# Two recurrence streams at a later scheduling priority, and one projection step moved, in a two-layer mixer kernel on one core

## Chip, cores and metric

The kernel runs on one core of a Trainium2 chip. The metric is device time in microseconds, one launch from start to end; "before" is 2253.34 us, the median of three runs (2252.33 to 2256.01). TensorE is called PE below, VectorE DVE, ScalarE ACT, GpSimd POOL and SyncE SP, as in the profile. Nearly all DMAs stand on SP's queue.

## What is computed

The reference is a diffusion backbone of two layers over 512 latent tokens with 256 context tokens ahead of them (768 in all), width 1024, in float32. Cut to what matters here:

```python
for l in range(2):
    h = modulate(rms_norm(x, g_norm1[l]), sh1, sc1)        # latent; hc the same for the context
    proj = h @ w_in[l]                                     # 3744 columns, split into three groups
    # A: latent attention (cq, ckv, kr), 4 heads; B: differential attention (dq, dk, dv), 4 heads
    # C: gated linear recurrence, 8 heads of 64, forward and backward:
    #    S_t = diag(f_t) S_{t-1} + k_t^T v_t ,  o_t = S_t^T q_t   (hf, hb -> f, k; hq -> q; hi -> v)
    x = x + gt1 * (concat(A, B, C * silu(hg)) @ w_out[l])
    x = x + gt2 * swiglu(modulate(rms_norm(x, g_norm2[l]), sh2, sc2))
    # layer 0 does the same for the context tokens, layer 1 does not
return rms_norm(x, g_final)
```

## The kernel before, in words

Products are made from pairs of high and low halves: `gemm` (line 190) issues three matmuls for each 128 rows of weights, weight high by activation high and low, weight low by activation high. Weights come by DMA into `wst`, ACT makes `whi` of it (line 97) and DVE `wlo` (line 100).

In each layer `phase_a` mixes the tokens, and then an FFN follows. `phase_a` is written as generators, which the loop at its end (lines 1036 to 1059) steps in turn by a table of due times:

- `stream_g` projects the columns in the steps of `G_ORDER[l]`: `t0` to `t3` (`trio`) project the forget and query columns of one pair of recurrence heads each and store them to `scr_z`; `h0`, `h1` project the recurrence's token-major inputs (`hi`, the values, line 493) for two pairs each and store them to `scr_v`; `q` and `d` belong to the differential attention; `g0` to `g3` are the output gates, `a4` to `a9` blocks of the modulation. Then it does the output projection (`m2` and `xT` loads, `g<-m` matmuls), whose first part needs the key `"h"`, which is set when the recurrences have ended.
- `stream_p` makes the operands of the latent attention, `stream_a` the attention itself: scores (line 764), a minimum per row on DVE (`mx`, line 768), the exponential on ACT, transposes (line 804), and the product with the values (line 817).
- `stream_h(0)` and `stream_h(1)`, called `h` and `i` in the table, compute the recurrence. Four pairs of heads go one after the other, the first head of a pair in `h` and the second in `i`. A pair loads its inputs from `scr_z` into `hin`, and goes through seven levels (`LEVELS`). Each level makes a masked copy `kz` of `KK` on ACT, twelve (in layer 1 eight) 64x64 score matmuls on PE (line 918, line 930 at the last level), two predicated copies of the scores into `sc` on DVE (line 963), and four products on `KK` and `QQ` on DVE (line 100), on which the next level of the same head stands. Then come transposes of `KK` (line 984), products with the values `hv` (line 990) and a scan over chunks, and the outputs `mixh` (line 1008). `KK`, `QQ` and `sc` have one buffer for each stream, so a pair can't begin before the one ahead of it has ended; the values of `h0` are needed only behind the levels.

The generators set the order in which instructions are recorded. A scheduler then orders each engine's queue: every instruction gets a number, `tc.cur_priority`, which grows by one with each; among instructions that it holds to be ready it takes the lowest number. Each engine runs its list in that order. The scheduler's idea of when something is ready is its own; the hardware waits by semaphores.

The program prints the functions of the change below.

Of the kernel before, what the change touches and what calls it, by code (L numbers as in the profile page):

```python
# [31 lines left out]
GROUPS = ((4, 4, 4, 4, 3, 3), (4, 4, 4, 4, 3, 3))  # L32
LEVELS = (1, 2, 4, 8, 16, 32, 64)
PRED = (1, 2, 4, 8, 16)
G_ORDER = ("t0 h0 q t1 d t2 h1 t3 a5 a4 g0 a8 a6 g1 a9 a7 g3 g2", "t0 t1 h0 t2 q d h1 t3 g0 g1 g3 g2")


PRM = ((40, 2, 2.1, 2, 1.2), (45, 1.8, 2.7, 2.2, 0.4))
# [15 lines left out]
LAG = 4  # L54
LOCK = 1
GB = 1
NSTEP = "011"


# [31 lines left out]
def build(tc, I, out):  # L91
# [304 lines left out]
    def hpair():  # L396
        return (hp.tile([128, KT, T], F32R, tag="hh", name="hh"), hp.tile([128, KT, T], F32R, tag="hl", name="hl"))
# [13 lines left out]
    def phase_a(l, h, fs):  # L411
# [92 lines left out]
        def stream_g():  # L504
# [72 lines left out]
            for i in range(2):  # L577
                steps[f"h{i}"] = partial(hi, i)
            for key in G_ORDER[l].split():
                yield from steps[key]()  # L580
# [152 lines left out]
        def stream_a(at):  # L733
# [47 lines left out]
            def finish(it):  # L781
# [10 lines left out]

                if "h" in done or "proj" in done and GB:
                    bank = cbank if "h" in done else gbank
# [240 lines left out]
        with ps:  # L1035
            vt = {"g": 0.0, "h": 0.0, "i": 0.0, "p": PRM[l][0], "a": 1e9}
            apool = ExitStack()
            gens = {"g": stream_g(), "h": stream_h(0), "i": stream_h(1),
                    "p": stream_p(apool.enter_context(tc.tile_pool(name=f"P{l}", bufs=1, reuse_waits="tile")))}
            stretch = dict(zip("ghipa", (PRM[l][i] for i in (1, 2, 2, 3, 4))))  # L1040
            while gens:
                k = min(gens, key=lambda n: vt[n])
                try:
                    c = next(gens[k])
                except StopIteration:
                    del gens[k]
                    if k == "a":
                        apool.close()
                        done.add("a")
                    if k == "p":  # L1050
                        apool.close()
                        gens["a"] = stream_a(apool.enter_context(tc.tile_pool(name=f"at{l}", bufs=1, reuse_waits="tile")))
                        vt["a"] = vt["p"]
                    continue
                if c == "wait":
                    vt[k] = min(vt[o] for o in gens if o != k) + 1e-3
                else:
                    vt[k] += c * stretch[k]
            apool.close()
# [3 lines left out]

    FIRST = {"q": [O_DQ, O_DQ + 128, O_DK], "t": [O_HF, O_HB, O_HQ]}[G_ORDER[0][0]]
    h = hpair()
# [114 lines left out]
    for l in range(DEPTH):  # L1180
# [3 lines left out]
        po = 0 if full else 256  # L1184
        with ExitStack() as fs:
            x, h2 = phase_a(l, h, fs)
            pbs.close()
            pq = fs.enter_context(tc.tile_pool(name=f"pq{l}", bufs=4, space=PSUM))
# [6 lines left out]
            def ada_next():  # L1195
                for ll, nb in [(0, 10), (0, 11)] + [(1, nb) for nb in range(12)]:
                    if f"{'ab'[ll]}{nb}" in " ".join(G_ORDER).split():
                        continue
# [217 lines left out]
            for n in GROUPS[l]:  # L1416
# [40 lines left out]
                for pcols in ((c,) for c in batches) if last else (parts,):  # L1457
# [13 lines left out]
                    if last:  # L1471
                        if full:
                            if pcols[0].start == 0:
# [3 lines left out]
                                h = hpair()  # L1477
                            norm = norm_mod(x, acc, a1, mod[1][:, 0:8, :], pcols[0], h, wp2, qbank,
                                            lambda: pf.tile([128, 512], F32, tag="f", name="f"), 4, THR if pcols[0] is B1 else "")
                            if pcols[0] is B2:  # L1480
                                for i, (slot, c0) in enumerate(((0, O_HF), (4, O_HB), (8, O_HQ))[:NBEG]):
                                    for _ in range(int(NSTEP[i])):
                                        next(norm)
# [47 lines left out]
```

## Time and profile before

| | value |
|---|---|
| median of three runs | 2253.34 us |
| the profiled execution | 2252.72 us |
| its span, first to last instruction | 2250.8 us |
| PE busy | 2062.0 us (92%) |
| PE weight loads busy | 1764.9 us (78%) |
| DVE busy | 1606.0 us (71%) |
| ACT busy | 1060.6 us (47%) |
| mean granted PE clock | 0.949 |

The span falls into a head (up to about 50 us), the mixing of layer 0 (to about 735), its FFN (to about 1318), the mixing of layer 1 (to about 1850) and its FFN. A view by stretches gives, for each engine, the busy time in that stretch and the number of instructions in brackets; behind them stand the granted PE clock (1.00 is 2.4 GHz, 0.50 is 1.2 GHz, a value between them a mixture), the busy share of the DMA engines and what they moved. Matmuls overlap in the records, so the busy time of PE is more than its work. One 64x64 fp32 matmul is two records.

### The profile page before, as it was taken

Reading aid. Unit: us, or ns where it says so; the run is one execution under the profiler, and the core shown is the slowest. Engines: PE = TensorE matmul, PEld = TensorE weight load, DVE = VectorE, ACT = ScalarE, POOL = GpSimd, SP = SyncE. Lnnn points to the kernel's source line nnn. Section 1 sums busy time; section 2 is a strip of 40 time slices with the busy share of each in tenths; the row PEclk is TensorE's granted clock in tenths of the full one; section 3 lists DMA queues with packets and bytes.
Section 4 is the critical chain, followed back from the end, with each engine's and each line's share of the span. In section 5 each row is a group of like instructions: output and inputs, shape, how many; then the busy total and the mean of one; then the engine's idle time right before and its main releaser. Section 6 shows DMA issues by size and latency. Waiting matters only on the chain.

```text
span 2250.8 us, 38089 instructions
## 1 busy us (share of the span) xinstructions
PE 2062.0 (92%) x14863; PEld 1764.9 (78%) x14863; DVE 1606.0 (71%) x3395; ACT 1060.6 (47%) x1888; POOL 13.2 (1%) x48
## 2 busy tenths in 40 slices
PE   6999999878889999999999999987998679999998
PEld 4887878656577888898999978766876568899997
DVE  5675587867466656687867777788578658777887
ACT  4443776565554322232323453545677444344443
POOL 0000000000000000000000000000000000000000
PEclk9999999878889999999999999998998789999999
DMA  9427643355684433544522342355654553333322
GB/s 310 135 70 176 183 117 116 88 150 158 197 251 136 150 103 113 154 133 140 159 67 70 85 140 83 104 125 140 163 148 127 157 161 104 99 95 107 100 87 69
DMA packets 321244, 296.52 MB, mean 132 GB/s; under 512 B 28875, under 2 KB 263721, under 8 KB 321065
## 3 DMA queue, kind: packets, MB, share of 16 engines
q1 hardware_dynamic: 321064, 294.10, 44.9%
q8 instruction: 117, 1.92, 0.4%
q14 instruction: 63, 0.51, 0.1%
HBM read 241.09 MB, written 52.95 MB: 131 GB/s over the span
## 4 chain that ended last, share of the span: by engine, by line
PE 64%; DVE 13%; ACT 6%; DMA 4%; issue 2%; SPq 0%; DVEq 0%; ACTq 0%
PE g L190 19%; PE q L190 18%; PE f L190 11%; PE b L764 3%; PE g L493 2%; DVE QQ L100 2%; DVE KK L100 2%; DVE sc L963 2%; PE c L918 1%; PE b L190 1%; PE b L817 1%; PE b L804 1%; ACT P L97 1%; DVE mx L768 1%; DMA q<-scr_d 1%
## 5 line engine op out<-in xcount | busy, mean ns | idle before, releaser
L97 ACT ACTIVATE whi<-wst 128x1024 fp32r<-128x1024 f32 (+2 forms) x248 | 225.3, 908 | 413.0 <-PE f L190 143.6
L100 DVE TENSOR_TENSOR wlo<-wst,whi 128x1024 fp32r<-128x1024 f32 (+2 forms) x248 | 255.9, 1034 | 72.3 <-ACT whi L97 67.5
L190 PE MATMUL q<-hh,whi 128*128 128x384 f32 (+1 forms) x708 | 223.6, 318 | 4.3 <-ACT whi L97 3.2
L190 PE MATMUL q<-hh,wlo 128*128 128x384 f32 (+1 forms) x708 | 221.5, 315 | 0.9 <-DVE wlo L100 0.9
L190 PE MATMUL q<-hl,whi 128*128 128x384 f32 (+1 forms) x708 | 221.9, 315 | 0.0
L190 PE MATMUL g<-hh,whi 128*128 128x512 f32 (+1 forms) x560 | 204.8, 367 | 14.4 <-ACT zt L97 6.5
L190 PE MATMUL g<-hl,whi 128*128 128x512 f32 (+1 forms) x560 | 201.0, 360 | 0.4 <-DVE hl L103 0.3
L190 PE MATMUL g<-hh,wlo 128*128 128x512 f32 (+1 forms) x560 | 199.6, 359 | 1.2 <-DVE wlo L100 1.2
L768 DVE TENSOR_REDUCE mx<-b 128x1 f32<-128x768 f32 (+1 forms) x120 | 101.1, 848 | 72.4 <-PE b L764 71.1
L190 PEld LDWEIGHTS q<-hh,whi 128*128 128x128 f32 x708 | 134.3, 191 | 14.2 <-ACT whi L97 6.7
L190 PE MATMUL f<-ah,whi 128*128 128x512 f32 (+1 forms) x380 | 137.2, 364 | 6.4 <-DVE xT L103 4.1
L190 PE MATMUL f<-ah,wlo 128*128 128x512 f32 (+1 forms) x380 | 136.0, 361 | 1.1 <-DVE wlo L100 1.1
L190 PE MATMUL f<-al,whi 128*128 128x512 f32 (+1 forms) x380 | 136.5, 361 | 0.0
L190 PEld LDWEIGHTS q<-hh,wlo 128*128 128x128 f32 x708 | 134.4, 191 | 2.5 <-DVE wlo L100 1.6
L190 PEld LDWEIGHTS q<-hl,whi 128*128 128x128 f32 x708 | 134.6, 191 | 1.2 <-issue 0.8
L190 PEld LDWEIGHTS g<-hh,whi 128*128 128x128 f32 x560 | 109.6, 196 | 32.1 <-ACT zt L97 8.0
L103 DVE SCALAR_TENSOR_TENSOR xT<-f,mod,xT 128x256 f32<-128x256 f32 (+1 forms) x164 | 85.8, 546 | 68.3 <-PE f L190 68.0
L190 PE MATMUL g<-m,whi 128*128 128x256 f32 (+1 forms) x512 | 117.7, 324 | 11.5 <-DMA m<-scr_m 9.4
L97 ACT ACTIVATE kz<-KK 64x384 f32<-64x384 f32 (+1 forms) x192 | 90.9, 475 | 73.6 <-DVE KK L100 35.1
L918 PEld LDWEIGHTS c<-QQ,kz 128*64 128x64 f32 x1920 | 74.0, 153 | 63.3 <-ACT kz L97 34.0
L918 PE MATMUL c<-QQ,kz 128*64 128x64 f32 x1920 | 87.3, 243 | 39.0 <-DVE sc L963 25.9
L190 PEld LDWEIGHTS g<-hh,wlo 128*128 128x128 f32 x560 | 108.8, 195 | 17.1 <-DVE wlo L100 2.3
(308 smaller groups left out, 5103.2 us busy)
## 6 DMA issues: line engine op xcount, KB each, us to landing
wst<-in_w_in_dram SPq DMA_DIRECT2D x58, 512.0 KB, 5.2
wa<-in_w_ada_dram SPq DMA_DIRECT2D x56, 512.0 KB, 3.6
wst<-in_w_out_dram SPq DMA_DIRECT2D x32, 512.0 KB, 4.3
wst<-in_w_ffn_down_dram SPq DMA_DIRECT2D x64, 256.0 KB, 2.9
wst<-in_w_ffn_gate_dram SPq DMA_DIRECT2D x26, 512.0 KB, 3.7
wst<-in_w_ada_dram SPq DMA_DIRECT2D x24, 512.0 KB, 4.7
hin<-scr_z SPq DMA_DIRECT2D x48, 192.0 KB, 3.9
k<-scr_k SPq DMA_DIRECT2D x16, 576.0 KB, 4.8
```

Source lines behind the costliest of these rows:

```text
L97: return S.activation(out=out, in_=in_, func=func, **kw)
L100: eng.tensor_tensor(out=out, in0=in0, in1=in1, op=op)
L103: return V.scalar_tensor_tensor(out=out, in0=in0, scalar=scalar, in1=in1, op0=op0, op1=op1)
L190: PE.matmul(out=o, lhsT=x[:, k, ms], rhs=y[:, k, cols], start=start and k == 0 and p == 0, stop=stop and k == nk - 1 and p == 2, skip_grou ...
L493: PE.matmul(out=o, lhsT=x[:, kk, tok], rhs=y[:, kk % 4, :], start=kk == 0 and p == 0, stop=kk == KT - 1 and p == 2)
L764: PE.matmul(out=s[:, 256 + k0:256 + k0 + kn], lhsT=qq[:, q0:q0 + 128], rhs=kk[:, k0:k0 + kn], start=p == 0, stop=p == len(passes) - 1)
L768: V.tensor_reduce(out=mx, in_=sv, axis=AX.X, op=ALU.min)
L804: PE.transpose(b[:, (kt - k0) * 128:(kt - k0 + 1) * 128], P[:, kt * 128:(kt + 1) * 128], ident)
L817: PE.matmul(out=o[e * 64:e * 64 + 64, :256], lhsT=it["v"][:, e, kt, :], rhs=u[e][:, kt, :], start=kt == 0, stop=kt == it["ntk"] - 1)
L918: PE.matmul(out=bv[e * 64:e * 64 + 64, i, :], lhsT=kz[:, cc], rhs=q[:, cc], start=True, stop=True)
L963: V.copy_predicated(out=sv, data=bv, mask=masks[:64, PRED.index(m), :].unsqueeze(1).to_broadcast([64, n, 64]))
```

## The change

The recurrences' generators `h` and `i` run with `cur_priority` raised by 200 for what they record, in both layers, so that 200 places' worth of other instructions recorded behind them go first where the scheduler holds both ready. When a generator ends, the exception skips the line that takes the 200 off again, so all that is recorded behind the end of `h`, and again of `i`, stands 200 further back as well. In layer 0's table, `h0` stands behind `d` and no longer behind `t0`, so `q`, `t1` and `d` go ahead of it.

```diff
-G_ORDER = ("t0 h0 q t1 d t2 h1 t3 a5 a4 g0 a8 a6 g1 a9 a7 g3 g2", "t0 t1 h0 t2 q d h1 t3 g0 g1 g3 g2")
+G_ORDER = ("t0 q t1 d h0 t2 h1 t3 a5 a4 g0 a8 a6 g1 a9 a7 g3 g2", "t0 t1 h0 t2 q d h1 t3 g0 g1 g3 g2")
...
+AHEAD = ({'h': -200, 'i': -200}, {'h': -200, 'i': -200})
...
                 k = min(gens, key=lambda n: vt[n])
                 try:
+                    p0 = tc.cur_priority
+                    tc.cur_priority = p0 - AHEAD[l].get(k, 0)
                     c = next(gens[k])
+                    tc.cur_priority += AHEAD[l].get(k, 0)
                 except StopIteration:
```

No instruction is added or removed but for 6 of 30 loads of an ACT table, which fall away with the new order. The line numbers of the changed kernel are 1 higher from line 57 on, and 4 higher behind the loop.

The order at three places follows (of each queue, the program's own list; names carry buffer numbers, "x12" is twelve in a row).

PE, layer 0, fourth pair of recurrence heads, in the middle of its levels, before (`QQ_5029` is the first head, `QQ_5056` the second; `kz8` and `kz16` are the levels of 8 and 16):

```order
L804 MATMUL b_5260<-ident_73,P_5148 128x128 x6
L764 MATMUL b_5268<-k_5244,q_5246 128x256
L764 MATMUL b_5268<-k_5244,q_5246 128x512
L918 MATMUL c_5350<-QQ_5029,kz8_1077 64x64 x12
L764 MATMUL b_5394<-k_5244,q_5246 128x256
L764 MATMUL b_5394<-k_5244,q_5246 128x512
L918 MATMUL c_5373<-QQ_5056,kz8_1077 64x64 x12
L190 MATMUL g_5456<-hh_95,whi_5427 128x256
L190 MATMUL g_5456<-hl_96,whi_5427 128x256
L918 MATMUL c_5496<-QQ_5029,kz16_1135 64x64 x12
L918 MATMUL c_5519<-QQ_5056,kz16_1135 64x64 x12
```

The same pair in the changed order (`QQ_4978` and `QQ_5153`):

```order
L919 MATMUL c_5357<-QQ_5153,kz2_788 64x64 x12
L311 MATMUL g_5689<-sel_76,zt_5687 128x2 x4
L304 MATMUL g_5767<-wst_5765,csil_84 32x512
L223 MATMUL b_5494<-blk_77,sq_5492 128x2 x2
L304 MATMUL g_5767<-wst_5765,csil_84 32x512
L304 MATMUL g_5767<-wst_5770,csil_84 32x512 x2
L919 MATMUL c_5517<-QQ_4978,kz16_1044 64x64 x12
L304 MATMUL g_5767<-wst_5774,csil_84 32x512 x2
L304 MATMUL g_5767<-wst_5778,csil_84 32x512 x2
L919 MATMUL c_5540<-QQ_5153,kz4_913 64x64 x9
L311 MATMUL g_5784<-sel_76,zt_5782 128x2 x4
L919 MATMUL c_5540<-QQ_5153,kz4_913 64x64 x3
```

Before, the two heads go side by side, level by level, with little between them; now the second head runs two levels behind the first, and work of other streams stands between nearly all groups.

SP, layer 0, where the first part of the output projection loads its inputs, before (`m2` are the mixers' outputs, `xT` the residual):

```order
L178 DMA wst_6652<-in_w_out_dram 128x8x128
L400 DMA m2_6656<-scr_m0 128x2x512 x2
L400 DMA k_6455<-scr_d0 96x2x768
L400 DMA q_6457<-scr_d0 96x2x256
L178 DMA wst_6654<-in_w_out_dram 128x8x128
L400 DMA zt_6414<-scr_n0 128x768
L400 DMA m2_6656<-scr_m0 128x2x512 x4
```

And in the changed order:

```order
L401 DMA k_6451<-scr_d0 96x2x768
L401 DMA q_6453<-scr_d0 96x2x256
L401 DMA scr_n0<-mixh_5792 128x768
L179 DMA wst_6935<-in_w_out_dram 128x8x128
L401 DMA zt_6410<-scr_n0 128x768
L401 DMA m2_6652<-scr_m0 128x2x512 x3
```

The first two loads of `m2` stood ahead of the last attention head's `k` and `q`; now all eight stand behind them, closer together, and behind the store of the last recurrence's output (`mixh`).

PE, layer 1, last pair of recurrence heads (`QQ_17047` first, `QQ_17110` second), around the level of 4, before:

```order
L764 MATMUL b_15959<-k_15914,q_15916 128x256
L764 MATMUL b_15959<-k_15914,q_15916 128x512
L918 MATMUL c_17346<-QQ_17110,kz4_13137 64x64 x8
L190 MATMUL g_17389<-hh_12393,wlo_17386 128x512
L190 MATMUL g_17389<-hh_12393,whi_17385 128x512
L190 MATMUL g_17389<-hl_12394,whi_17385 128x512
```

and in the changed order (`QQ_17043`, `QQ_17106`):

```order
L805 MATMUL b_16209<-ident_73,P_16162 128x128 x6
L919 MATMUL c_17269<-QQ_17106,kz2_12972 64x64 x8
L919 MATMUL c_17288<-QQ_17043,kz4_13133 64x64 x8
L919 MATMUL c_17342<-QQ_17106,kz4_13133 64x64 x8
L919 MATMUL c_17361<-QQ_17043,kz8_13173 64x64 x8
L765 MATMUL b_16240<-k_16236,q_16238 128x256
```

Before, each group stood alone, with 22 rows of projections and attention between the two heads' groups of the level of 4; now the pair has moved back, and four of its groups follow each other.

## Rows read from the trace of the kernel before

**Rows 1.** The page: span and busy time of PE.

```profile
span 2250.8 us, 38089 instructions
PE 2062.0 (92%) x14863; PEld 1764.9 (78%) x14863; DVE 1606.0 (71%) x3395; ACT 1060.6 (47%) x1888; POOL 13.2 (1%) x48
```

**Rows 2.** View by stretches, both mixing stages: busy time of each engine, clock, DMA.

```profile
core 0: us, PE busy (x) PEld busy (x) DVE busy (x) ACT busy (x) POOL busy (x), PEclk, DMA share, GB/s
...
269.10:312.50 43.40, 39.73 (x476) 32.69 (x473) 41.84 (x81) 34.15 (x62) 0.58 (x4) 1.00 0.42 108
312.50:372.30 59.80, 57.22 (x524) 49.35 (x525) 40.99 (x121) 41.46 (x89) 0.00 (x0) 0.94 0.48 136
372.30:410.50 38.20, 30.50 (x409) 26.10 (x404) 36.72 (x79) 22.23 (x47) 0.59 (x4) 0.92 0.18 59
410.50:477.70 67.20, 58.69 (x471) 42.37 (x471) 46.78 (x132) 45.26 (x82) 0.00 (x0) 0.88 0.52 145
477.70:537.30 59.60, 46.05 (x440) 35.00 (x436) 49.75 (x98) 30.30 (x56) 0.58 (x4) 0.70 0.34 100
537.30:592.00 54.70, 50.69 (x414) 35.68 (x412) 28.28 (x81) 31.57 (x59) 0.00 (x0) 0.97 0.64 187
592.00:631.00 39.00, 32.44 (x153) 21.03 (x153) 19.14 (x35) 20.52 (x38) 0.00 (x0) 0.82 0.90 267
...
1353.40:1385.70 32.30, 27.79 (x307) 22.84 (x302) 30.65 (x80) 14.58 (x31) 0.58 (x4) 0.98 0.20 61
1385.70:1457.10 71.40, 70.54 (x542) 59.05 (x542) 44.03 (x116) 31.52 (x64) 0.00 (x0) 0.96 0.34 96
1457.10:1493.90 36.80, 34.72 (x317) 26.24 (x318) 34.06 (x73) 16.61 (x34) 0.58 (x4) 0.99 0.61 142
...
1528.60:1631.20 102.60, 93.73 (x794) 80.69 (x794) 71.07 (x154) 60.74 (x109) 0.58 (x4) 0.92 0.55 144
1631.20:1689.30 58.10, 55.10 (x419) 42.20 (x421) 43.64 (x115) 43.10 (x74) 0.00 (x0) 1.00 0.56 155
1689.30:1736.10 46.80, 38.46 (x346) 29.42 (x342) 41.21 (x100) 32.44 (x60) 0.58 (x4) 0.85 0.43 127
```

**Rows 3.** Timeline of PE, 395 to 412 us: start, time, instruction, wait before it.

```profile
398.10 0.92 PE L918 MATMUL c<-QQ,kz 128*64 128x64 f32 x24
398.95 0.50 PE L190 MATMUL g<-hl,whi 128*128 128x512 f32 x1
...
401.60 0.92 PE L918 MATMUL c<-QQ,kz 128*64 128x64 f32 x24 [1.91 <-DVE sc L963]
404.93 1.55 PE L918 MATMUL c<-QQ,kz 128*64 128x64 f32 x24 [2.41 <-DVE sc L963]
408.97 1.55 PE L918 MATMUL c<-QQ,kz 128*64 128x64 f32 x24 [2.50 <-ACT kz L97]
```

**Rows 4.** DVE groups, 262 to 592 us: busy, mean ns of one, idle before them.

```profile
L100 DVE TENSOR_TENSOR KK<-KK,tot 64x384 f32<-64x384 f32 x72 | 39.7, 551 | 3.3 <-ACT kz L97 1.4 <-PE c L930 0.4
L100 DVE TENSOR_TENSOR QQ<-QQ,tot 64x384 f32<-64x384 f32 x72 | 39.5, 548 | 0.5
L963 DVE COPY_PREDICATED sc<-masks,c 64x384 f32<-64x384 uint8 x60 | 35.2, 587 | 1.7
L768 DVE TENSOR_REDUCE mx<-b 128x1 f32<-128x768 f32 x32 | 30.4, 955 | 15.6 <-PE b L764 15.1
...
L100 DVE TENSOR_TENSOR wlo<-wst,whi 128x1024 fp32r<-128x1024 f32 x10 | 12.2, 1222 | 6.3 <-ACT whi L97 6.2
```

**Rows 5.** The chain that ended last: start, time, what.

```profile
457.71 2.70 DMA scr_z<-zt
460.97 8.04 DMA hin<-scr_z
...
569.78 2.74 PE b L817 x24
...
1957.41 4.32 PE q L190 x36
...
1999.17 21.92 PE f L190 x96
```

## Prediction

> **What bounds the kernel now.** I read the page first. PE is busy for 2062.0 of 2250.8 us [rows 1], so at first sight order can give little. But the records of matmuls overlap, and a half clock makes them longer, so I priced PE's list instead: 21.92 us for 96 matmuls of 512 columns is 0.228 us each, 4.32 us for 36 of 256 columns is 0.120, and 2.74 us for the 12 value products of two heads (24 records) is 0.23 [rows 5]. Twelve 64x64 scores take 0.92 us with their tail [rows 3]; I take 0.06 each, and price other shapes by their columns in the same way. "Priced us" below are sums of such prices along PE's list. By them the whole list is some 1810 us, so about 440 us of the span are waits, slower clock and latency, and they lie mostly in the two mixing stages.
>
> Second, the view by stretches, cut where the score groups of the recurrence pairs stand: from the first group of the level of 1 to the last of the level of 32. In layer 0 these are 269.1 to 312.5 us (second pair), 372.3 to 410.5 (third) and 477.7 to 537.3 (fourth) [rows 2]. In the third, DVE is busy for 36.72 of 38.2 us and PE's list holds 24.5 priced us; in the fourth it is 49.75 of 59.6, with 27.2 priced us, and the granted clock is 0.70 [rows 2]. In layer 1 the pairs' stretches show the same: 30.65 of 32.3 us, 34.06 of 36.8, and 41.21 of 46.8 for the last [rows 2]. So while a pair goes through its levels DVE bounds the kernel, and PE is under-used. Outside them it is the other way: between 312.5 and 372.3 us PE is busy for 57.22 of 59.8 us, and DVE for 40.99 [rows 2].
>
> Third, the timeline shows how. PE waits 1.91, 2.41 and 2.50 us ahead of three score groups in a row, each time for the recurrence's own work on DVE or ACT [rows 3]. One level of one head costs DVE two predicated copies of 0.587 us, two products on `KK` of 0.551 and two on `QQ` of 0.548 [rows 4], 3.4 us in all; fourteen of them are 47 us, though a pair's first and last lie partly outside the cut.
>
> **The change, part by part.** It adds no work, so what counts is how much other work stands between a pair's groups. From the two orders, between the first and the last group of line 918: the second pair of layer 0 has 34.0 priced us before and 33.2 now, the third 24.5 and 40.2, the fourth 27.2 and 56.0. The fourth has 117 matmuls of other streams before and 281 now. With them DVE work moves in. Summing DVE's rows in the same pieces of the order by their mean durations (a maximum is 0.955 us, a `wlo` 1.222 [rows 4], and so on) gives 44.8 us and 48.9 for the second pair, 40.3 and 61.4 for the third, 53.4 and 72.7 for the fourth.
>
> How long does such a stretch take? Before, the sums of 44.8, 40.3 and 53.4 took 43.4 (269.1 to 312.5), 38.2 and 59.6 us [rows 2]: 1.02 us for 1 us of DVE sum over the three. So now 50, 63 and 74 us: together 46 us more. (PE's work in them, 33 to 56 priced us, is below that.) Against it 43.7 priced us leave the rest of the stage. What they cost there is the largest unknown. In the stretch from 312.5 to 372.3, 48.9 priced us take 59.8, which is 1.22 us for one; from 410.5 to 477.7, 41.0 take 67.2, or 1.64, and from 537.3 to 631 57.2 take 93.7, or 1.64 [rows 2]. At 1.22 they give back 53 us, a net of -7; at 1.64 72 us, a net of -26. The slower stretches hold waits that don't go with the work: a store of 2.70 us and a load of 8.04 ahead of the fourth pair [rows 5], DMA at 0.90 of its engines from 592 to 631 [rows 2]. I take -17, the middle.
>
> Three edits cost nothing by this count. The first pair of layer 0 grows from 40.1 to 44.4 priced us and from 43.9 to 51.2 of DVE, and what it gains it pays. `h0` moved behind `d`: its matmuls run at PE's pace wherever they stand; the first pair's outputs now wait for it (place 219 in PE's priced list, before 115), and the second pair begins at 235 and not 207. That is 28 priced us later, under which `q`, `t1` and `d` run, which had to run anyway. Six fewer ACT table loads lie on an engine that is busy for 41 of 60 us at most there [rows 2].
>
> The DMAs of the output projection move on SP's queue: eight loads of `m2` (0.52 MB each) and four of `xT` (0.79) now begin behind the end of the recurrence and stand together. 7.3 MB at the 267 GB/s of the stretch 592 to 631 [rows 2] are 27 us, less than the work listed beside them before, but first matmuls follow 6 priced us behind the first load. Between nothing and half of those 27 us can show; I take +4, nearer to nothing, since attention is still listed beside them.
>
> In layer 1 the same sums give: first pair, priced 23.3 to 52.0, DVE 32.4 to 40.0; PE bounds it now, at the 1.12 of the stretch 1385.7 to 1457.1 (64 priced us in 71.4), so 58 us for 32.3 [rows 2], against 32 us of work that left the rest: -6. Second pair, 30.0 to 24.3, DVE 35.8 to 36.1: the stretch stays at 37 and 6 us of work go back outside: +6. Third, 80.9 to 77.4 priced: it took 102.6 [rows 2] and shrinks as its work does: 0. Last pair, 28.3 to 20.6, DVE 44.9 to 35.2: 46.8 us become 37, and 7.7 priced us at the 1.19 of 1631.2 to 1689.3 (49 in 58.1) [rows 2] come back as 9: 0. The sum is 0, within 12 to either side: the two terms of 6 may each stand without the other, and the last pair as much again.
>
> Sum: -17 + 4 + 0 = -13 us on the profiled execution's 2252.72, which is 0.6 under the median of the runs: **2240 us**. What is late next: in layer 0 DVE through the third and fourth pair, then the loads of `m2`.
>
> **The rivals.** *The levels become slower by what stands between them (slower).* If a level's PE wait and its DVE work don't overlap with the other head's, each of the fourteen groups costs its share of the filler plus the chain. The chain alone is 38.2/14 = 2.7 us [rows 2]; the filler is 40.2/14 = 2.9 in the third pair and 56.0/14 = 4.0 in the fourth. 14 x 5.6 is 78 us where I took 63, and 14 x 6.7 is 94 where I took 74: 35 us more, a net of +22, 2275 us. It decides from two fifths of that on, where my 13 us are used up. For it: PE does stand still at the head of its list with a 512-column matmul next in line [rows 3]. Against it: the second head now runs two levels behind the first, so the two seldom want DVE at once. The Trainium skill ("PSUM — Partial Sum Buffer", section "Engine vs sequencer instructions") says that the queues of DVE and ACT are strict FIFO and that matmuls start in program order. By that a score group put behind other work waits for all of it even when its operands are there, which is this rival, and the waits of [rows 3] agree with the rule. Chance 0.24.
>
> *Nothing moves.* The moved work gives back only 1.22, 7 us, the loads cost 4, and layer 1 has part of its second pair's 6 and less from its first: about 0, so 2253 us. For it: DVE was at 36.72 of 38.2 us [rows 2], and a bound engine gains nothing by company. The Trainium skill ("Perfetto Trace Analysis", section "Identifying the Most-Contended Engine") tells to judge PE by its weight loads and to work on the engine with the highest occupancy; that would be PE, at 78% of weight loads against DVE's 71% [rows 1], whose work the change leaves as it is, so by the rule alone the time stays. The stretches speak against the average: DVE leads in some and PE in others. Chance 0.13.
>
> *All of it comes back.* At 1.64 layer 0 gains 26 us, the loads cost nothing, layer 1 gains the 6 of its first pair: 2221 us. For it: the stretch at clock 0.70 [rows 2] would get its clock back with work between its groups. Against it: the waits for DMA. Chance 0.13.
>
> **How the numbers follow.** 0.2% of the time, 4.5 us, is about what a measurement can tell here. The forecast (2230 to 2248) has 0.50; with the third rival that is 0.63 for faster. The second rival is 0.13 for the same, the first 0.24 for slower. The lower end lies under the third rival by the 12 us of layer 1 and the 4 of the loads: 2205. The upper end reaches to half of the first rival's way, from 2253 to 2275: 2264. Left out are about 0.06 below and 0.13 above.
>
> **What would show it right or wrong.** Right: the fourth pair's stretch in layer 0 takes 65 to 80 us at a clock over 0.85 with DVE over 0.85; the third takes 55 to 68; layer 0's FFN begins 8 to 22 us earlier; layer 1's mixing takes as long as before within 12. Wrong: a fourth stretch of 90 us or more with DVE under 0.75 (the first rival), or PE waiting over 10 us for `m2` ahead of the output projection, or layer 1's last pair taking its old 47 us and beginning 15 later.

## The result, and the profile after

The changed kernel takes 2282.51 us (median of four runs, 2277.8 to 2285.25) against 2252.84 before (2243.22 to 2256.01): a ratio of 1.0137, with a 95% interval of 1.0102 to 1.0172. It is 30 us slower. The forecast was 2240, with 2264 as its upper end.

The profiled execution after is the one of 2283.19 us. Its page begins so:

```profile
span 2281.4 us, 38042 instructions
PE 2127.6 (93%) x14863; PEld 1798.7 (79%) x14863; DVE 1604.4 (70%) x3395; ACT 1053.3 (46%) x1880; POOL 13.2 (1%) x48
```

Against [rows 1] DVE and ACT do what they did, but PE's records are 65.6 us longer for the same 14863 instructions. PE did not wait longer (153.8 us without a record, 188.8 before); its work became longer.

Where does the loss lie? The first matmul of layer 0's second FFN product (`f`) starts at 822 us before and at 821 after, so in sum the mixing of layer 0 costs what it did. In layer 1 the same matmul starts at 1924 before and at 1954 after. The net loss is in layer 1's mixing. The view by stretches of the changed kernel, cut as in [rows 2] at each pair's first and last score group (the four pairs of layer 1, then the second to fourth of layer 0):

```profile
core 0: us, PE busy (x) PEld busy (x) DVE busy (x) ACT busy (x) POOL busy (x), PEclk, DMA share, GB/s
1361.20:1440.20 79.00, 78.93 (x497) 61.28 (x496) 38.59 (x83) 20.41 (x40) 0.58 (x4) 0.96 0.26 74
...
1500.30:1538.70 38.40, 30.40 (x296) 23.71 (x292) 34.49 (x68) 15.14 (x29) 0.58 (x4) 0.91 0.51 127
...
1569.80:1668.80 99.00, 91.74 (x790) 79.57 (x790) 67.42 (x151) 60.90 (x108) 0.58 (x4) 0.92 0.50 133
...
1741.70:1779.30 37.60, 29.12 (x316) 22.13 (x313) 34.02 (x74) 25.00 (x48) 0.58 (x4) 0.86 0.40 109
...
312.60:358.10 45.50, 41.98 (x468) 34.05 (x464) 42.45 (x92) 29.51 (x67) 0.58 (x4) 0.96 0.33 103
...
404.10:461.90 57.80, 50.73 (x555) 40.89 (x554) 54.41 (x131) 35.54 (x75) 0.58 (x4) 0.91 0.33 88
...
493.50:589.10 95.60, 84.79 (x733) 62.42 (x732) 67.73 (x150) 56.09 (x95) 0.58 (x4) 0.87 0.59 170
```

The row to look at is the first. Layer 1's first pair took 32.30 us before [rows 2] and takes 79.00 now, with PE busy for 78.93 of them. It holds 52 priced us; the forecast was 58. PE waits for no engine in it. (DVE waits there for score groups, 31.2 us in all; PE, busy throughout, sets the time.) PE's timeline in that stretch shows what it does:

```profile
1393.70 0.33 PE L919 MATMUL c<-QQ,kz 128*64 128x64 f32 x2
1393.96 0.39 PE L494 MATMUL g<-wlo,hh 128*128 128x256 f32 x1
1394.28 0.33 PE L919 MATMUL c<-QQ,kz 128*64 128x64 f32 x2
1394.53 0.39 PE L494 MATMUL g<-whi,hl 128*128 128x256 f32 x1
1394.85 0.33 PE L919 MATMUL c<-QQ,kz 128*64 128x64 f32 x2
```

The scheduler hasn't put these score groups behind other work as wholes. It has dealt their matmuls out one by one (a matmul is two records) between matmuls of a projection. From one score matmul to the next, with one matmul of 256 columns between, it is 0.57 us (1394.28 to 1394.85). By the prices of the prediction, 0.120 and 0.06, it should be 0.18. So each return trip costs 0.39 us beyond the work. The form in the rows tells a difference between the two: `128*64` (64 of the array's columns in use) against `128*128`.

Another pair of lines in the same trace alternates as finely, in layer 0, both in the form `128*128`:

```profile
366.99 0.27 PE L985 MATMUL c<-ident,KK 128*128 128x128 f32 x1
367.02 0.36 PE L494 MATMUL g<-whi,hl 128*128 128x256 f32 x1
367.23 0.27 PE L985 MATMUL c<-ident,KK 128*128 128x128 f32 x1
367.25 0.36 PE L494 MATMUL g<-whi,hh 128*128 128x256 f32 x1
367.45 0.27 PE L985 MATMUL c<-ident,KK 128*128 128x128 f32 x1
...
1387.19 0.87 PE L238 MATMUL b<-ident,rs_y 128*128 128x128 f32 x6
1387.82 0.48 PE L191 MATMUL b<-hh,whi 128*128 128x512 f32 x1
```

Here it is 0.23 us from one to the next, which is just 0.12 for the 256 columns and 0.11 for the 128 (six matmuls of that form in a row take 0.63 us, 1387.19 to 1387.82). Alternation between two streams alone costs nothing here.

So I counted, on PE's list in each kernel, the **runs of 64-wide tiles**: unbroken series of matmuls of lines 918, 930, 990, 1008 and the other two 64-wide lines (240, 817), each of which is one return trip. Before there are 99 in layer 0 and 80 in layer 1; after, 183 and 183. In layer 1's first pair it is 10 before and 60 after. 187 more at 0.39 are 73 us.

### The profile page after: what moved, and what is told of

The parts are those of the page before. It is cut to its first block, busy times and chain, and to the rows that moved or that the text cites. A ratio compares the mean times of both kernels' runs of the same rounds, so it can differ in the third digit from the quotient of the medians.

```text
span 2281.4 us, 38042 instructions
## 1 busy us (share of the span) xinstructions
PE 2127.6 (93%) x14863; PEld 1798.7 (79%) x14863; DVE 1604.4 (70%) x3395; ACT 1053.3 (46%) x1880; POOL 13.2 (1%) x48
## 5 line engine op out<-in xcount | busy, mean ns | idle before, releaser
L919 PE MATMUL c<-QQ,kz 128*64 128x64 f32 x1920 | 105.2, 240 | 27.4 <-ACT kz L98 13.6
L919 PEld LDWEIGHTS c<-QQ,kz 128*64 128x64 f32 x1920 | 82.0, 148 | 61.5 <-ACT kz L98 20.9
L191 PEld LDWEIGHTS g<-hl,whi 128*128 128x128 f32 x560 | 108.4, 194 | 18.0 <-issue 2.1
```

The costliest lines, as they stand in the source:

```text
L191: PE.matmul(out=o, lhsT=x[:, k, ms], rhs=y[:, k, cols], start=start and k == 0 and p == 0, stop=stop and k == nk - 1 and p == 2, skip_grou ...
L919: PE.matmul(out=bv[e * 64:e * 64 + 64, i, :], lhsT=kz[:, cc], rhs=q[:, cc], start=True, stop=True)
```

## The experiments

Theory A is that these return trips are the loss. Theory B is the prediction's first rival: a group put behind other work in PE's queue waits for it. All runs are medians; the ratio is against runs of before on the same chip.

**The parts alone.** Three kernels undo part of the change (shown against the changed kernel):

```diff
order_only
-AHEAD = ({'h': -200, 'i': -200}, {'h': -200, 'i': -200})
+AHEAD = ({'h': 0, 'i': 0}, {'h': 0, 'i': 0})
ahead_l0
+AHEAD = ({'h': -200, 'i': -200}, {'h': 0, 'i': 0})
ahead_l1 (and layer 0's old table)
+AHEAD = ({'h': 0, 'i': 0}, {'h': -200, 'i': -200})
```

> Layer 0's table as changed, but no priority offset (AHEAD 0 in both layers). Theory A (what costs is that TensorE alternates between the recurrence's 128x64 tiles and the 128x128 tiles of other streams; a lone score pair between two matmuls of 256 columns costs about 0.4 us more than its own 0.06, as layer 1's first pair showed): the list has 101 runs of 64-wide tiles in layer 0 before something else follows, against 99 before and 183 with the whole change; so no cost of that kind, 2245 to 2260. Theory B (a level is slower because its group waits behind filler in the queue): no filler moved, 2245 to 2260 too. If the table alone cost or gave more than 10 us, both would have left out a part.

Measured: 2263.84 us, ratio 1.0050 (1.0033 to 1.0068), against 2252.73. The table alone costs 11 us, more than either theory had room for.

> The offset in layer 0 alone (with layer 0's changed table); layer 1 records and runs in the order of before. The changed kernel's layer 0 ended at the time of before's, so theories A and B expect 2249 to 2257, the whole loss of 30 us being layer 1's. If the loss came from what layer 0 leaves to layer 1 (loads or weights that come later), it would stay at 2275 or more.

Measured: 2245.71 us, ratio 0.9977 (0.9958 to 0.9995). Layer 1 without the offset loses nothing; the result is even a little under the expected band. It is 18 us under `order_only`, so in layer 0 the offset gains more than the breaks cost.

> The offset in layer 1 alone, layer 0's table as before. Theory A: 103 more runs of 64-wide tiles in layer 1 (183 against 80) at about 0.4 us each are 41 us, of which some lies where TensorE isn't the bound: 2278 to 2290. Theory B: the same 30 us by waits, 2278 to 2290; it tells A and B from any effect of layer 0, not from each other.

Measured: 2291.35 us, ratio 1.0149 (1.0113 to 1.0184), 1 us above the band. Its first pair in layer 1 takes 83.0 us, with the same 60 runs. So the loss is the offset in layer 1, and nothing that layer 0 hands over.

**The suspected cost taken away.** `whole_after` ties the groups: from its second matmul on, a group has a priority far ahead, so nothing comes between. This is the scores' part; the last level, the products with the values and the outputs are tied in the same way.

```diff
+WHOLE = 100000
...
                             PE.matmul(out=bv[e * 64:e * 64 + 64, i, :], lhsT=kz[:, cc], rhs=q[:, cc], start=True, stop=True)
+                            if i + e == 0:
+                                tc.cur_priority -= WHOLE
+                    tc.cur_priority += WHOLE
```

> The changed kernel, but from its second matmul on each group of the recurrence (scores, products with the values, outputs) gets a priority far ahead, so that nothing comes between a group's matmuls; the groups' own places behind other work stay as the change made them. The list has 94 runs of 64-wide tiles in layer 0 and 76 in layer 1, against 183 and 183. Theory A: layer 1 gives back its 30 us or more, layer 0 up to 89 x 0.4 = 36 us where TensorE is the bound: 2215 to 2250, 2230 most likely. Theory B: the groups wait behind the same filler as before, so 2272 to 2290.

Measured: 2199.68 us, ratio 0.9758 (0.9736 to 0.9780). That is 83 us under the changed kernel and 53 under the kernel before, more than A expected and below its band. B falls as the account of the loss: just as much other work stands between the groups (45.6, 31.7, 40.2 and 55.9 priced us in layer 0's four pairs, against 44.4, 33.2, 40.2 and 56.0 in the changed kernel), and the kernel is the faster for it. 83 us for 196 fewer runs is 0.42 each, close to the 0.39 read from the timeline. By the end of each layer's last `f` product (1304 and 2270 us in the changed kernel, 1271 and 2189 in this one) layer 0 gives back 33 us for 89 fewer runs and layer 1 49 for 107, so layer 0 had a loss too, which a gain had hidden. Its PE timeline in layer 1's first pair:

```profile
1328.14 0.28 PE L192 MATMUL g<-hh,whi 128*128 128x256 f32 x1
1328.35 0.69 PE L920 MATMUL c<-QQ,kz 128*64 128x64 f32 x16
1328.97 0.39 PE L192 MATMUL g<-hl,whi 128*128 128x256 f32 x1
1329.19 0.28 PE L192 MATMUL g<-hh,wlo 128*128 128x256 f32 x1
```

A whole group of eight costs 0.71 us here (1328.14 to 1328.97, less 0.12 for the 256 columns). Eight matmuls dealt out singly cost 8 x 0.45 = 3.6. And the same stretches as above (the second, third and fourth pair of layer 0, and layer 1's first):

```profile
300.20:339.60 39.40, 36.53 (x461) 30.21 (x457) 37.85 (x82) 27.24 (x63) 0.58 (x4) 1.00 0.34 107
...
379.90:438.70 58.80, 51.80 (x554) 42.12 (x553) 54.50 (x130) 35.04 (x75) 0.58 (x4) 0.88 0.33 85
...
469.90:556.60 86.70, 76.57 (x730) 56.14 (x728) 67.83 (x151) 55.98 (x95) 0.58 (x4) 0.92 0.59 172
...
1325.40:1380.90 55.50, 55.50 (x489) 48.76 (x488) 38.35 (x84) 20.44 (x41) 0.58 (x4) 1.00 0.39 112
```

Layer 1's first pair takes 55.5 us with 12 runs, for 79.0 with 60. 48 x 0.39 is 19 us of those 23.5.

**Is it the tying itself?** `whole_before` ties the groups of the kernel before, `whole_order` adds the changed table, `whole_ahead` the offset with the old table.

> The kernel before, with the same tying of each group's matmuls as in the run whole_after and nothing else (no offset, old table). The list has 165 runs of 64-wide tiles, against 179 before and 170 in whole_after. Theory A (each such run costs about 0.4 us): 14 x 0.4 = 6 us less, 2240 to 2254; the rest of whole_after's 53 us then comes from the offset. Rival: tying the groups is itself what helps and the offset gives nothing: 2195 to 2210.

Measured: 2248.22 us, ratio 0.9978 (0.9962 to 0.9993), as A expected. The kernel before had few broken groups: tying them removes 14 runs of 179.

> Tied groups and the changed table of layer 0, no offset. 161 runs of 64-wide tiles against 181 in order_only (2264 us). Theory A: 20 x 0.4 = 8 us less than order_only, 2248 to 2264. If it comes to about 2200, the offset isn't what makes whole_after fast.

Measured: 2257.26 us, ratio 1.0009 (0.9992 to 1.0025), inside the band.

> Tied groups and the offset of 200 in both layers, with layer 0's old table. 166 runs of 64-wide tiles. The changed table alone cost 11 us (order_only), so if table and offset add up, 2185 to 2196; if the moved step only helps or hurts without the offset, 2195 to 2206.

Measured: 2225.14 us, ratio 0.9878 (0.9863 to 0.9892). A miss: neither 2190 nor 2200. With tied groups the offset gives 23 us without the changed table (2248 to 2225) and 58 with it (2257 to 2200). So the table, which costs 9 to 11 us alone, gives 25 with the offset. I can say where it shows: layer 0's fourth pair begins at 490 us in `whole_ahead` and at 470 in `whole_after`. Why, no run tells.

**Width or alternation?** `wide_after` is the changed kernel with layer 1's scores as 128-wide tiles:

```diff
...
-                            PE.matmul(out=bv[e * 64:e * 64 + 64, i, :], lhsT=kz[:, cc], rhs=q[:, cc], start=True, stop=True)
+                            if full:
+                                PE.matmul(out=bv[e * 64:e * 64 + 64, i, :], lhsT=kz[:, cc], rhs=q[:, cc], start=True, stop=True)
+                            else:
+                                PE.matmul(out=bw[:, i, e, :], lhsT=kz[:, c * 128:c * 128 + 128], rhs=q[:, cc], start=True, stop=True)
...
```

> The changed kernel, groups not tied, but layer 1's score matmuls take all 128 columns of a chunk as weights (128x128 tiles, the half that isn't used is not read); still fp32, still 64 columns streamed. The list has them even more broken up than the changed kernel (139 runs of scores in layer 1, against 115). If what costs is the change between 64- and 128-wide tiles, a lone score pair between two 256-column matmuls takes 0.2 to 0.3 us instead of 0.57, and layer 1's first pair falls from 79 us to 55 to 65: 2245 to 2268 in all. If it is the change between accumulations, banks or number formats, the pair still takes 0.57 and the time is 2278 to 2300.

Measured: 2308.01 us, ratio 1.0246 (1.0215 to 1.0277), outside both bands, and the first pair takes 69.6 us. Yet its PE timeline answers the question:

```profile
1360.84 0.33 PE L924 MATMUL c<-QQ,kz 128*128 128x64 f32 x2
1360.98 0.36 PE L191 MATMUL g<-hh,whi 128*128 128x256 f32 x1
1361.18 0.33 PE L924 MATMUL c<-QQ,kz 128*128 128x64 f32 x2
1361.32 0.36 PE L191 MATMUL g<-hl,whi 128*128 128x256 f32 x1
1361.52 0.33 PE L924 MATMUL c<-QQ,kz 128*128 128x64 f32 x2
1361.66 0.36 PE L191 MATMUL g<-hh,wlo 128*128 128x256 f32 x1
1361.86 1.89 PE L924 MATMUL c<-QQ,kz 128*128 128x64 f32 x16
1363.59 1.45 PE L223 MATMUL b<-ones,tmp 128*128 128x1 f32 x12
```

A lone score between two 256-column matmuls now takes 0.34 us (1360.84 to 1361.18), not 0.57. The numbers are still fp32 and the accumulations still change, so it is the width. But a block of eight takes 1.73 us (1361.86 to 1363.59) and not the 0.62 of the rows of `whole_after` (1328.35 to 1328.97): 0.22 each. 0.12 and 0.22 are the 0.34, so a lone wide score has no surcharge at all. The kernel is slower because every whole block became 1.1 us longer, which I had left out of the expectation. It also splits the 0.39: a 64-wide matmul in a group of eight takes 0.08 (0.62/8), a 128-wide one alone 0.22. If a lone 64-wide one needs as long as a wide one (an estimate from this row), some 0.15 of the 0.39 is the lost company of its neighbours, and some 0.24 the change of width, out and back. The Trainium skill ("TensorEngine Tiling (Array Packing)", section "Tiling Modes") says that a change of tiling mode drains TensorE, and that different tiles can compute in parallel. The wide score without a surcharge agrees with the first, and the block of eight, faster with 64-wide tiles, agrees with the second; the page has no price for the change.

**The suspected cost added.** `broken200` is the kernel before with no offset for the generators, but with each group's matmuls behind the first set 200 places back (the diff of `whole_after` with -200 for `WHOLE`).

> The kernel before with no offset for the generators and the old table; but within each group of the recurrence every matmul behind the first gets a priority 200 places later, so that the groups are broken up. The list has 396 runs of 64-wide tiles against 179 before; little else moves (the third, fourth and last pairs keep their 25 to 29 priced us of work between first and last group). Theory A (a run costs about 0.4 us, in full where TensorE is the bound): 217 x 0.4 = 87 us at most, half of it where a pair waits for the vector engine anyway: 2295 to 2340. Rival (the breaks cost nothing; the changed kernel lost by where its groups stand): 2245 to 2270.

Measured: 2349.42 us, ratio 1.0436 (1.0410 to 1.0462), against 2251.59. 98 us for 217 more runs is 0.45 each on average, but the average hides two unlike layers: by the end of each layer's last `f` product layer 0 loses 24 us for 120 more runs (0.20 each) and layer 1 72 for 97 (0.74 each). Breaking the groups makes the kernel before slower. It isn't a clean test of the price, though: between the first and the last score group of layer 1's first pair now stand 324 records of PE's other work, against 106 before, about as in the changed kernel (303), so work has moved here too. The clean pair is the changed kernel and `whole_after` (303 and 295 such records). What layer 1 lost beyond the price no run parts; that a broken group also ends later, and DVE waits for it (31.8 us in that pair), is a likely part.

**Versions that go on.** All with tied groups and the changed table: the 200 taken off again where a generator ends, an offset of 400, and one of 800.

```diff
whole_noleak
                 except StopIteration:
+                    tc.cur_priority += AHEAD[l].get(k, 0)
```

> whole_after (2200 us) with one more line: when a recurrence's generator ends, the 200 places are taken off again, so that what is recorded behind its end has its old priority. The lists differ only around the recurrences' ends and the output projections (629 of 9737 rows of TensorE). If the leftover offset does nothing that counts: 2194 to 2206. If it holds back the output projection's work: 2180 to 2194. If it helps (attention first): 2206 to 2220.

Measured: 2207.72 us (2198.35 to 2208.66), ratio 0.9790 (0.9768 to 0.9813); `whole_after` had 0.9758 (0.9736 to 0.9780). The median lies just inside the band of "it helps", but the intervals overlap: the leftover offset makes no clear difference.

> Tied groups, changed table, offset 400 in place of 200. 171 runs of 64-wide tiles, as many as whole_after's 170. If what gains is that TensorE has other work between a recurrence's groups, more of it gains no more once the vector engine bounds the stretches: 2190 to 2215. If the recurrences now end too late for the output projection behind them: 2215 to 2250.

Measured: 2198.83 us, ratio 0.9752 (0.9730 to 0.9774), the same as with 200. The sameness is a sum of two differences: in the profiled executions layer 0's last `f` product ends 16 us earlier than in `whole_after` (1255 against 1271), and layer 1 takes 17 us longer from there (935 against 918). An offset of 400 in layer 0 and 200 in layer 1 was not run.

> The same with an offset of 800; 150 runs of 64-wide tiles. The point at which the recurrences end too late should be passed: 2210 to 2260. If it stays within 10 us of whole_400, the offset's size doesn't count beyond 200.

Measured: 2256.59 us, ratio 1.0011 (0.9995 to 1.0027). The gain is gone. By the profiled executions 37 of the 60 us lost against `whole_400` lie in layer 0 and 23 in layer 1. The recurrences do end later: the last score of layer 0's fourth pair ends at 584 us, against 539 with 400, and that of layer 1's last pair 501 us behind layer 0's last `f` product, against 458. PE's longest wait between 1700 and 1960 us is for the loads of layer 1's output projection (engine, line, what it waited for; total us, times, longest; `whole_800`, then the kernel before between 1740 and 1920):

```profile
PE g L192 <- DMA m<-scr_m: 12.5, 1, 12.5
...
PE g L190 <- DMA m<-scr_m: 8.1, 1, 8.1
```

It is only 4 us longer than before, so it isn't the loss, and what the late recurrences hold back stays open. An offset of 200 to 400 with tied groups is the best found, 53 us faster than the kernel before.

## Why the prediction was wrong, point by point

**The step that failed** is the first paragraph of the prediction: "Twelve 64x64 scores take 0.92 us with their tail [rows 3]; I take 0.06 each". That is a price for scores in whole groups, and it takes nothing for the group itself. The prediction then summed priced work between a pair's first and last group and never asked how many pieces the groups came in. The order shown ahead of it even has a group as nine, four others, three. The sum lacked a term: 187 more runs of 64-wide tiles, +73 us at 0.39, and 83 as measured by removing 196 of them. A reader can check such a thing before any run: [rows 3] show a group of twelve at 0.92 us, so 0.06 each leaves about 0.2 us that belongs to a group and not to its matmuls. That is half of the 0.39 that a lone score cost, but 187 times 0.2 is 37 us, which would already have turned the forecast of -13 round.

**The gain was under-sized.** With the broken groups out of the way, offset and table give 2199.68 against `whole_before`'s 2248.22, that is 49 us, not 13. In the profiled executions it is 46: by the end of each layer's last `f` product (1296 and 2235 us in `whole_before`, 1271 and 2189 in `whole_after`) 25.5 of it is layer 0's, where I had -17 + 4, and 20.5 layer 1's, where I had 0. So the direction was right: offset and table do gain; that they gain by other work between the groups fits, and was not isolated. Tying alone gave 5 us in the kernel before (0.9978 of 2252.84). So the change is -5, -49 and +83, from before by way of the two tied kernels; these steps add up to the 30 by construction and test nothing further.

**The stretches.** Of the seven forecasts, three came out in layer 1 (38.4 us for 37; 99.0 for 102.6 x 77.4/80.9 = 98; 37.6 for 37) and two nearly in layer 0 (45.5 for 50, 57.8 for 63). Two failed. Layer 1's first pair took 79.0 for 58; tied it takes 55.5, so the price by work was right; of the other 23.5 the breaks explain 19 by the price and the clock some 2.5 (below). Layer 0's fourth pair took 95.6 for 74. It has 29 runs, 18 when tied, which explains 4 us by the price and 9 by the run (86.7); the 13 us left over have no run of their own and stay open. In the tied kernel PE is without a record for 10.1 us of that stretch (86.70 less 76.57) and the granted clock is 0.92; DVE waits there for score groups for only 1.6 us, so the first rival's wait isn't it. Layer 0's first pair, costed at nothing, took 58.3 us for 46.9 before, with 21 runs for 12; tied it takes 54.0.

**What stood under "would show it".** Layer 0's FFN was to begin 8 to 22 us earlier; its first `f` product began 1 us earlier. The third pair's 55 to 68 us came out (57.8), and so did the fourth's clock (0.87 for over 0.85). The fourth pair's stretch was to be 65 to 80 us with DVE over 0.85; it is 95.6 with DVE at 67.73/95.6 = 0.71, which was the sign of the first rival. Layer 1's mixing was to stay within 12; it is 30 longer.

**The rivals.** The first gave 2275, and the time is 2282.51; but its mechanism is not the cause. It said that groups wait behind filler, and `whole_after` keeps the filler and gains 83 us. Its 94 us for layer 0's fourth pair came near (95.6, and 86.7 tied), but it also wanted 78 for the third, which took 57.8. Its number came out near by chance. "Nothing moves" and "all of it comes back" are out.

**The edits costed at nothing.** The moved `h0` is not free: alone it costs 11 us (`order_only`), with the offset and tied groups it gives 25. The sum had no way to see that, since it priced each edit apart. The loads of the output projection, costed at 4, cost nothing: PE waits for `m` in layer 0's output projection for 0.7 us in all between 640 and 745 us, against 1.3 before.

## What to carry to other kernels

When a change lets a scheduler interleave streams, price the pieces and not only the work: count on PE's list how often the tile's width changes, and read the cost of one change from a timeline row where a lone matmul of one width stands between two of another. If small tiles must yield to other work, let them yield as whole groups. And a change that loses can hold a gain: offset and table together were worth 49 us here once the groups were tied.

## What the runs showed of the hardware

A lone 64-wide fp32 matmul between 128-wide ones cost 0.39 us beyond both works; the same alternation among 128-wide tiles cost nothing (0.23 us for 0.12 and 0.11), and a 128-wide score had no surcharge either (0.34 for 0.12 and 0.22). Whole groups of eight 64-wide scores ran at 0.08 us each, blocks of eight 128-wide ones at 0.22.

Behind the first finely broken stretch of the changed kernel the granted clock fell to half (0.51 is almost all 1.2 GHz). The view by stretches and PE's timeline there:

```profile
1374.00:1380.00 6.00, 6.00 (x28) 4.46 (x29) 3.55 (x14) 0.00 (x0) 0.44 (x3) 0.51 0.17 54
...
1374.58 0.63 PE L191 MATMUL g<-hl,whi 128*128 128x512 f32 x1
1375.01 0.63 PE L191 MATMUL g<-hh,wlo 128*128 128x512 f32 x1
...
1380.52 0.40 PE L191 MATMUL g<-hl,whi 128*128 128x512 f32 x1
1380.76 0.39 PE L191 MATMUL g<-hh,wlo 128*128 128x512 f32 x1
```

From 1374.6 to 1379.8 us a matmul of 512 columns comes every 0.43 us, then again every 0.23. It cost about 2.5 us. PE's records had no gap ahead of that; from 1361 to 1372 us it had been alternating. Whether the alternation lowered the clock is open. For it: the first pair of layer 1 had 1.00 throughout in the tied kernel (1325.4 to 1380.9 us) and in `wide_after` (1355.1 to 1424.7), and in `ahead_l1`, broken as finely as the changed kernel, the clock was 0.50 from 1375 to 1385. Against it: the changed kernel's second and longer alternation, from 1393.7 us on, kept 1.00 (1400.0 to 1440.2), and `broken200` kept 1.00 behind its first (1414.6 to 1435.0) and had 0.86 in its second (1447.0 to 1503.8).
